# Forgetting attention with the keys' running sums used as loaded: the causal mask from one GpSimd selection per tile, and the row of reciprocal sums stored from ScalarE's queue

## The chip, the core and the metric

The kernel runs on one core of one Trainium2 chip. The metric is the device time of one execution in microseconds (us); the kernel before takes 1107.3 us (median of three runs, 1104.75 to 1107.84).

The core has five engines, each with an instruction queue of its own: TensorE (PE in the profile, with its weight loads as PEld), VectorE (DVE), ScalarE (ACT), GpSimd (POOL) and SyncE (SP), which here only issues DMAs. Each engine works through its queue in order, and semaphores tie the queues together.

## The reference, cut to what matters

The program is one decoder block on a sequence of 1024 tokens of width 1024: an input projection, attention with a forget gate beside a branch of chunked spatial gating (gMLP), an output projection, then a gated feed-forward layer with a short convolution. The change lies in the attention, which has 8 heads of dimension 64:

```python
c = jnp.cumsum(log_f, axis=1)                 # log_f = log_sigmoid(forget gate)
logits = einsum('bqhd,bkhd->bhqk', qi, k) * scale
logits = logits + ci[..., None] - c_k         # running sum of the query minus that of the key
logits = jnp.where(causal, logits, -inf)
p = softmax(logits, axis=-1)
out = einsum('bhqk,bkhd->bqhd', p, v)
```

The softmax of a row does not change when one number is added to the whole row, so the term `ci` of the query can be left out of the computation without changing `p`.

## The kernel before

All large products are split into three passes of a high and a low part, and the projections use a Strassen-like scheme. One list of stages runs from top to bottom: input projections (to about 215 us of the profiled execution), attention together with the projection of the gMLP branch (about 222 to 410 us), then the feed-forward layer, in which TensorE runs without a pause until the end. Instructions of different stages are interleaved on the engines by a scheduler that works from the dependences; the code below says what depends on what, not the final order on each engine.

What the change touches, with the lines of the profile:

- **Constants, lines 124 to 131.** `ident` is a 128x128 identity in float32, `identb` its bfloat16 copy made by VectorE (line 127), `maskb` a bfloat16 tile that holds 3e38 above the diagonal and 0 elsewhere (a memset and one GpSimd selection, line 130). `maskb` is also used once in `forget` to build a triangular matrix.
- **`forget_sums`, lines 492 to 520.** It works out the running sums of the forget gates. `z` ends up as minus log_f, so the sums are minus the running sums of the reference. They are put into `ncq` (tokens on partitions, line 517), transposed by TensorE (line 518), copied out of PSUM by VectorE (line 519) into `rows` and stored by SP to `ncd` in DRAM (line 520), one row of 1024 numbers for each head. In the traces the instructions of this stage that go to VectorE and ScalarE are recorded with line 43, that of a helper which keeps their order.
- **`att_head`, lines 702 to 788**, called for heads 0 to 7. For a head it loads queries and keys (`A`, `B`, `B2`: high and low parts) and the row of running sums, spread over 128 partitions (`nck`, line 708). `nck` and `B2` are two halves of one tile with the tag `x2`, of which there are two; the loads of a head therefore wait until the head two before it has done with the tile.
- Inside, `i` runs over four pairs of query tiles, `j` over the two tiles of a pair. A query tile `j` has n = 128*(j+1) keys. GpSimd first fills the tile `t` (128 x n) with the running sum of the query minus that of the key (line 725). Then, in chunks of up to 512 keys: TensorE multiplies queries and keys into PSUM in two passes (lines 733, 734); in the chunk with the diagonal a third small matmul adds `maskb` (line 736, identity in bfloat16 as stationary operand); VectorE adds `t` to the PSUM and takes the running minimum in one instruction (line 738; the products carry a minus sign, so that a minimum takes the place of the softmax's maximum). ScalarE then takes the exponential of the whole tile with its sum (line 741).
- After that, the tile is transposed by TensorE in 128x128 blocks (line 755), split into high and low part by ScalarE and VectorE (lines 756, 757), and multiplied by the values (line 765). At four points of a head `filler` puts in products of the gMLP branch (lines 808 to 810), which keep TensorE busy while the softmax runs; they are used up in the third head (head 2).
- **The end of a head, lines 774 to 788.** The reciprocal of the 1024 row sums `rs` is transposed by TensorE (777), copied by ScalarE to `rt` (778), stored by SP to `rsd` in DRAM (779), and loaded back as one row spread over 64 partitions (780). For every second head the attention output is multiplied by that row (786; GpSimd for the first three pairs of heads, VectorE for the last) and split again (787, 788).

SP issues nearly all DMAs in one queue. An instruction that waits there holds up the loads behind it. GpSimd in this stretch does the fills of line 725, the low parts of the weights of the output projection (line 163), and lines 786 and 788.

## Time and profile before

| | |
|---|---|
| median of three runs | 1107.3 us (1104.75 to 1107.84) |
| the profiled execution | 1106.7 us |
| its span from first to last instruction | 1104.9 us |
| granted TensorE clock, mean over the span | 0.994 |
| instructions | 14551 |
| HBM traffic | 142 GB/s over the span |

How to read the rows. "L733 PE MATMUL" is a matmul of line 733. A group of instructions has its count (x96), its busy time in us, the mean duration of one in ns, and the idle time of the engine just ahead of it with what ended that idle time. The durations of matmuls overlap: they are pipelined, one starts well before the one ahead has ended, so that the distance from start to start, and not the duration, is what a matmul costs TensorE. The chain of waits is followed back from the last instruction: at each step to the instruction or transfer that released it. In rows of stretches the columns are the stretch in us, its length, and for each engine busy time and number of instructions, then the granted clock, the share of the DMA engines and GB/s.

### The profile page before, as it was taken

The page shows a single profiled execution, that of the slowest core. Times are in us where ns is not written, and L with a number is a line of the kernel's source. Part 1 is how long each engine was busy: PE and PEld are TensorE (multiplying, and loading weights), DVE is VectorE, ACT ScalarE, POOL GpSimd, SP SyncE. Part 2 cuts the span into 40 slices and gives each one's busy share as a digit, 9 for nine tenths or more (in the row PEclk, how much of TensorE's full clock was granted, in tenths as well). Part 3 has the DMA queues.
Part 4 walks back from the last instruction along what each step waited for, and adds up shares of the span by engine and source line. Part 5 has one row for each costly group of instructions (what it writes and reads, how often), then busy time and mean ns, then how long its engine had stood idle before and what let it go on. Part 6 is the DMA issues. An engine that isn't in the chain of part 4 may idle for free.

```text
span 1104.9 us, 14551 instructions
## 1 busy us (share of the span) xinstructions
PE 1076.5 (97%) x5077; PEld 882.7 (80%) x5077; DVE 899.3 (81%) x1357; ACT 572.7 (52%) x990; POOL 267.0 (24%) x205
## 2 busy tenths in 40 slices
PE   9999998999999999998999999999999999999997
PEld 6888787787887788776888888888888888888886
DVE  5985799774679868999899999999898875898774
ACT  5656543454468766663434444444435444444653
POOL 0002233133146441334333332323332000000000
PEclk9999999999999999999999999999999999999999
DMA  9242366846575335313223132323321899433342
GB/s 336 87 152 78 97 167 175 256 128 212 190 218 173 96 111 180 110 60 122 86 105 133 67 124 96 115 77 112 127 87 48 268 314 334 131 96 98 128 135 98
DMA packets 64714, 158.19 MB, mean 143 GB/s; under 512 B 7672, under 2 KB 7936, under 8 KB 64640
## 3 DMA queue, kind: packets, MB, share of 16 engines
q1 hardware_dynamic: 64480, 156.73, 43.8%
q8 instruction: 40, 0.66, 0.3%
q10 hardware_dynamic: 160, 0.53, 0.1%
q14 instruction: 34, 0.28, 0.1%
HBM read 114.95 MB, written 42.27 MB: 142 GB/s over the span
## 4 chain that ended last, share of the span: by engine, by line
PE 68%; DVE 8%; ACT 2%; DMA 2%; issue 2%; POOL 1%; SPq 0%; ACTq 0%; POOLq 0%; DVEq 0%
PE k L1195 18%; PE qa L1005 10%; PE qd L1005 10%; PE qc L1005 9%; PE qb L1005 5%; PE pb L765 3%; PE pb L755 2%; PE ps L260 2%; PE pf L808 1%; PE pf L809 1%; PE pf L810 1%; DVE whb L163 1%; DMA x<-ncd 1%; PE ps L733 1%; PE ps L734 1%
## 5 line engine op out<-in xcount | busy, mean ns | idle before, releaser
L1195 PE MATMUL k<-whb,wha 128*128 128x512 f32 x924 | 209.7, 389 | 0.0
L1195 PEld LDWEIGHTS k<-whb,wha 128*128 128x128 f32 x924 | 173.4, 188 | 36.1
L1005 PE MATMUL qa<-xB,wha 128*128 128x512 f32 x528 | 130.5, 397 | 4.4 <-DVE wha L163 4.4
L1005 PE MATMUL qc<-xT,whb 128*128 128x512 f32 x540 | 130.2, 390 | 1.3 <-DVE xT L936 1.3
L1005 PEld LDWEIGHTS qa<-xB,wha 128*128 128x128 f32 x528 | 101.0, 192 | 26.4 <-DVE wha L163 5.3
L1005 PEld LDWEIGHTS qc<-xT,whb 128*128 128x128 f32 x540 | 101.1, 188 | 23.2 <-DVE xT L936 1.7
L157 ACT CAST wha<-sg 128x512 fp32r<-128x512 f32 x77 | 47.9, 622 | 99.5 <-PE k L1195 85.8
L157 ACT CAST whb<-sg 128x512 fp32r<-128x512 f32 x85 | 52.0, 616 | 71.6 <-PE qc L1005 69.5
L163 DVE TENSOR_TENSOR wha<-sg,wha 128x512 fp32r<-128x512 f32 x77 | 52.8, 687 | 41.2 <-ACT wha L157 41.1
L163 DVE TENSOR_TENSOR whb<-sg,whb 128x512 fp32r<-128x512 f32 x85 | 62.9, 742 | 9.1 <-ACT whb L157 8.9
L1005 PE MATMUL qd<-xB,whb 128*128 128x512 f32 x264 | 63.9, 389 | 0.1
L1005 PE MATMUL qd<-xT,whb 128*128 128x512 f32 x264 | 63.4, 389 | 0.0
L765 PE MATMUL pb<-pt,V 128*128 128x256 f32 (+1 forms) x320 | 59.0, 299 | 3.4 <-ACT pt L756 2.7
L1005 PE MATMUL qb<-xT,whb 128*128 128x512 f32 x252 | 61.0, 389 | 1.0 <-DVE whb L163 1.0
L756 ACT CAST pt<-pb 128x512 fp32r<-128x512 f32 (+1 forms) x80 | 41.2, 543 | 38.6 <-PE pb L755 37.8
L1005 PEld LDWEIGHTS qd<-xB,whb 128*128 128x128 f32 x264 | 49.6, 188 | 10.8 <-issue 0.5
L757 DVE TENSOR_TENSOR pt<-pb,pt 128x512 fp32r<-128x512 f32 (+1 forms) x80 | 48.3, 633 | 12.2 <-ACT pt L756 11.9
L893 POOL TENSOR_TENSOR sg<-sg,raw 128x512 f32<-128x512 f32 x21 | 42.5, 2023 | 64.5 <-issue 63.4
L1005 PEld LDWEIGHTS qd<-xT,whb 128*128 128x128 f32 x264 | 49.5, 188 | 10.3
L765 PEld LDWEIGHTS pb<-pt,V 128*128 128x128 f32 x320 | 47.2, 190 | 13.1 <-ACT pt L756 8.2
L892 POOL TENSOR_TENSOR sg<-raw 128x512 f32<-128x512 f32 x21 | 30.6, 1457 | 110.0 <-DVE whb L163 98.1
L1005 PEld LDWEIGHTS qb<-xT,whb 128*128 128x128 f32 x252 | 47.2, 188 | 11.1 <-DVE whb L163 1.4
(381 smaller groups left out, 2347.9 us busy)
## 6 DMA issues: line engine op xcount, KB each, us to landing
raw<-wup SPq DMA_DIRECT2D x44, 512.0 KB, 3.6
sg<-hx SPq DMA_DIRECT2D x77, 256.0 KB, 2.8
hx<-hs SPq DMA_DIRECT2D x44, 256.0 KB, 2.0
hx<-ca SPq DMA_DIRECT2D x33, 256.0 KB, 2.0
xT<-wdn SPq DMA_DIRECT2D x28, 256.0 KB, 4.9
raw<-wqk SPq DMA_DIRECT2D x8, 512.0 KB, 3.9
qd<-G SPq DMA_DIRECT2D x16, 256.0 KB, 4.0
kd<-G SPq DMA_DIRECT2D x16, 256.0 KB, 3.2
```

Source lines behind the costliest of these rows:

```text
L157: act.copy(h, src)
L163: return eng.tensor_tensor(out=l, in0=src, in1=f32(h), op=ALU.subtract)
L260: pe.matmul(banks[m], xs(n, xi, k)[:, ms], w[:, wi, :], start=(first and k == 0 and c == 0), stop=(k == 3 and c == 2), skip_group_check=True)
L733: pe.matmul(ps[:, 0:e - c], A[:, qs], B[:, c:e], start=True, stop=False)
L755: pe.transpose(ptr[:, c:c + P], tj[jj][:, k * P:(k + 1) * P], ident)
L756: act.copy(pt[:, 0, 0:w], ptr[:, 0:w])
L757: dve.tensor_tensor(out=pt[:, 1, 0:w], in0=ptr[:, 0:w], in1=f32(pt[:, 0, 0:w]), op=ALU.subtract)
L765: pe.matmul(po[:, oo:oo + n], lhs, pt[:, s, o:o + n], start=(k == 0 and s == 0), stop=(s == 1 and half))
L892: pool.tensor_tensor(out=s[0], in0=a21, in1=a22, op=ALU.add)
L893: pool.tensor_tensor(out=s[1], in0=s[0], in1=a11, op=ALU.add)
L1005: pe.matmul(ps, w[:, wi, ks], xb[:, xi, k, :], start=(first and n == 0), stop=(n == 11), skip_group_check=True)
L1195: pe.matmul(banks[bk + m], xh[:, xi, ms], wh[:, wi, :], start=(first and p_ == 0 and n == 0), stop=(p_ == NP - 1 and n == 2), skip_group_c ...
```

## The change

Three edits.

1. The running sums of the keys enter the softmax as they are loaded. `forget_sums` writes its sums to `z` instead of `ncq`, and the copy out of PSUM moves from VectorE to ScalarE, where it also turns the sign (scale -1). The row in DRAM is then already what has to be added to the product, and the query's term is left out.
2. GpSimd's fill is replaced by one selection (`affine_select`) per query tile. It writes only the chunk that has the diagonal (columns c0 to n, with c0 = 0 for j < 4 and 512 for j >= 4): the running sums where the key is not after the query, 3e38 elsewhere. VectorE reads this chunk from `t` and the other chunk, which j >= 4 have, straight from the loaded row `ck`. The small matmul with `maskb` is gone, and so are `identb` and `ncq`.
3. The store of `rt` to `rsd` is issued by ScalarE instead of SP.

```diff
-    identb = cst.tile([P, P], BF16, name="identb")
-    dve.tensor_copy(identb, ident)
...
-        dve.tensor_tensor(out=ncq, in0=v3(ps[:, 64:128]), in1=run, op=ALU.add)
-        pe.transpose(ps[0:64, 192:320], ncq.rearrange("p h t -> p (h t)"), ident)
-        dve.tensor_copy(rows, ps[0:64, 192:320])
+        dve.tensor_tensor(out=v3(z), in0=v3(ps[:, 64:128]), in1=run, op=ALU.add)
+        pe.transpose(ps[0:64, 192:320], z, ident)
+        act.activation(rows, ps[0:64, 192:320], AF.Copy, scale=-1.0)
...
-                pool.tensor_scalar(out=t, in0=nck[:, 0:n], scalar1=-1.0, scalar2=ncq[:, h, j:j + 1],
-                                   op0=ALU.mult, op1=ALU.add)
+                c0 = (j // 4) * 512
+                pool.affine_select(out=t[:, c0:n], in_=ck[:, c0:n], pattern=[[-1, n - c0]], compare_op=ALU.is_ge,
+                                   fill=BIG, base=j * P - c0, channel_multiplier=1)
...
-                    last = e == n
...
-                    pe.matmul(ps[:, 0:e - c], A[:, qs], B2[:, c:e], start=False, stop=not last)
-                    if last:
-                        pe.matmul(ps[:, e - c - P:e - c], identb, maskb, start=False, stop=True)
+                    pe.matmul(ps[:, 0:e - c], A[:, qs], B2[:, c:e], start=False, stop=True)
...
-                    dve.tensor_tensor_reduce(out=t[:, c:e], in0=ps[:, 0:e - c], in1=t[:, c:e], scale=1.0,
+                    dve.tensor_tensor_reduce(out=t[:, c:e], in0=ps[:, 0:e - c], in1=(t if c == c0 else ck)[:, c:e], scale=1.0,
...
-        sp.dma_start(out=rsd[h], in_=rt)
+        act.dma_start(out=rsd[h], in_=rt)
```

The scheduler's order changes with it in places. On GpSimd the four selections of head 5's first two pairs now stand ahead of the multiplication of line 786 for the second pair of heads, where the four fills stood behind it. On SP the load of line 780 for head 3 now stands behind the first two loads of head 6, and that for head 4 behind the first load of head 7.

More of the change, by code (lines that the diff above doesn't have):

```diff
@@ L138, in block_kernel @@
     ss1 = cst.tile([P, 8], F32, name="ss1")
-    ncq = cst.tile([P, 8, 8], F32, name="ncq")
     qd = drm.tile([8, 2, 64, 1024], F32, name="qd")
@@ L704, in att_head @@
         ab, nb = sb("x1", [P, 2, 1024], F32R), sb("x2", [P, 2, 1024], F32R)
-        A, B, nck, B2 = ab[:, 0, :], ab[:, 1, :], f32(nb[:, 0, :]), nb[:, 1, :]
+        A, B, ck, B2 = ab[:, 0, :], ab[:, 1, :], f32(nb[:, 0, :]), nb[:, 1, :]
         sp.dma_start(out=f32(A), in_=qd[h].rearrange("s d t -> (s d) t"))
         sp.dma_start(out=f32(B), in_=kd[h].rearrange("s d t -> (s d) t"))
-        sp.dma_start(out=nck, in_=ncd[h:h + 1, :].to_broadcast((P, 1024)))
+        sp.dma_start(out=ck, in_=ncd[h:h + 1, :].to_broadcast((P, 1024)))
         sp.dma_start(out=f32(B2[0:64, :]), in_=kd[h, 1])
```

## The prediction

> **What bounds the kernel now.** I read the head of the page first, then the attention stage in three stretches, then the chain of waits in each.

> ```profile
> span 1104.9 us, 14551 instructions
> PE 1076.5 (97%) x5077; PEld 882.7 (80%) x5077; DVE 899.3 (81%) x1357; ACT 572.7 (52%) x990; POOL 267.0 (24%) x205
> ```

> TensorE is busy 97% of the span and GpSimd 24%: work taken from TensorE can shorten the kernel, work taken from GpSimd only where something waits for GpSimd. The edits lie in the attention, so this stage decides.

> ```profile
> 222.00:318.00 96.00, 95.01 (x531) 76.54 (x529) 60.51 (x144) 47.25 (x99) 36.50 (x41) 1.00 0.56 173
> 318.00:340.00 22.00, 19.99 (x147) 16.99 (x146) 18.61 (x51) 16.27 (x40) 7.35 (x10) 1.00 0.88 269
> 340.00:400.00 60.00, 56.96 (x398) 49.40 (x399) 50.54 (x135) 50.65 (x111) 36.85 (x35) 0.97 0.34 108
> ```

> In the first 96 us TensorE is busy 95.01 us, VectorE 60.51 and ScalarE 47.25: a plain TensorE bound, with the gMLP products as filling. In the next 22 us the DMA engines are at 0.88, TensorE misses 2 us. In the last 60 us TensorE misses 3 us, while VectorE and ScalarE are each busy 50.5 us: the softmax's chain through all engines. What sets the end shows in the chain, one row by line for each stretch, in order:

> ```profile
> by line: PE pf L808 14.2%; PE pf L809 14.0%; PE pf L810 13.6%; PE pb L765 13.6%; PE pb L755 10.1%; PE ps L733 6.2%; PE ps L734 5.3%; POOL whl L163 5.1%; PE pb L680 4.2%; PE pb L667 1.7%; PE pb L666 1.7%; PE pb L665 1.5%; DVE pt L757 1.5%; P
> by line: DMA x<-ncd 47.9%; DVE t L738 11.5%; issue 8.9%; DVE pt L757 8.2%; POOL t L725 4.5%; ACT H L741 3.8%; DVE H L772 3.1%; PE pb L765 3.1%; POOL H L725 2.3%; ACT pt L756 2.2%; SPq L707 1.9%; PE ps L734 1.6%; ACT t L741 1.2%; PE ps L736
> by line: PE pb L765 25.0%; PE pb L755 15.4%; POOL H L786 7.6%; PE ps L734 6.7%; PE ps L733 6.4%; DMA H<-rsd 5.9%; ACT pt L756 5.0%; DVE pt L757 4.9%; issue 3.9%; POOL H L725 3.5%; DVE t L738 2.4%; DVE H L772 2.2%; DMA rsd<-t 2.0%; ACT G L78
> ```

> First stretch: almost all TensorE. Second: half is the load of head 4's running sums, and TensorE hardly appears. Third: the four TensorE lines shown make 25.0 + 15.4 + 6.7 + 6.4 = 53.5%.

> **The change, part by part. The 64 mask matmuls.** Their group, and where they lie in the same stretches (instructions of line 736 alone):

> ```profile
> L736 PE MATMUL ps<-maskb,identb 128*128 128x128 bf16 x64 | 14.7, 230 | 0.0
> 222.00:318.00 96.00, 5.26 (x23) 2.21 (x23) 1.00 0.56 173
> 318.00:340.00 22.00, 2.98 (x13) 1.25 (x13) 1.00 0.88 269
> 340.00:400.00 60.00, 6.46 (x28) 2.79 (x28) 0.97 0.34 108
> ```

> The 14.7 us are durations, which overlap. A start-to-start reading needs one place in order of time, and two rows for spacing without a mask:

> ```profile
> 249.09 0.34 PE L734 MATMUL ps<-x,x 128*128 128x384 f32 x1
> 249.27 0.23 PE L736 MATMUL ps<-maskb,identb 128*128 128x128 bf16 x1
> 249.31 0.48 PE L733 MATMUL ps<-x 128*128 128x512 f32 x1
> 249.63 0.40 PE L734 MATMUL ps<-x,x 128*128 128x512 f32 x1
> ...
> 232.52 0.39 PE L809 MATMUL pf<-whl,G 128*128 128x512 f32 x1
> 232.75 0.40 PE L810 MATMUL pf<-whl,G 128*128 128x512 f32 x1
> ...
> 243.61 0.93 PE L755 MATMUL pb<-ident,H 128*128 128x128 f32 x7
> ...
> L755 PE MATMUL pb<-ident,H 128*128 128x128 f32 x80 | 12.8, 274 | 0.3 <-DVE H L772 0.3
> ```

> With the mask, the stretch from L734 to the next L734 is 0.54 us. Without it, L734 takes 0.18 (to 249.27) and the 512-column L733 0.23 (spacing of the gMLP products): 0.41. The mask costs 0.13 us, though the matmul behind it starts only 0.04 later: the rest appears as 0.32 instead of 0.23 on that next one, whose weights have no long matmul to be loaded under. The seven transposes give the same size: (0.93 - 0.27)/6 = 0.11 us each, 0.27 being the duration of one, from the last row. Bounds per mask: 0.04 (its own start spacing) and 0.23 (its duration); I take 0.13, which is measured across both neighbours.

> First stretch: 23 x 0.13 = 3.0 us, counted in full. Second: 13 masks, counted at nothing; the 10.54 us DMA below hides them, and what TensorE finishes earlier it waits longer. Third: 28 x 0.13 = 3.6, of which the 53.5% TensorE share gives 1.9. Together 4.9; with full cover lost or won, 3.0 to 8.3.

> [...]

> **GpSimd's selections.**

> ```profile
> L725 POOL TENSOR_SCALAR t<-x,ncq 128x896 f32<-128x896 f32 (+3 forms) x32 | 32.0, 1012 | 70.0 <-PE pb L755 39.7 <-PE ps L260 20.1 <-PE ps L736 10.2
> L725 POOL TENSOR_SCALAR H<-x,ncq 128x128 f32<-128x128 f32 (+3 forms) x32 | 16.6, 535 | 24.9 <-DMA x<-ncd 18.9 <-PE ps L734 6.0
> L658 POOL TENSOR_SCALAR_AFFINE_SELECT pt<-pt 128x1024 f32<-128x1024 f32 x1 | 1.6, 1552 | 0.0
> L130 POOL TENSOR_SCALAR_AFFINE_SELECT maskb<-maskb 128x128 bf16<-128x128 bf16 x1 | 0.3, 292 | 0.0
> ```

> The fills cost 48.6 us. A selection takes 292 ns at 128 columns and 1552 at 1024, so 1.41 ns a column: 292, 472, 652, 832 for the four widths, 16 of each, 36.0 us. Widths are now at most 512, so the long tiles gain and the 384 and 512 ones lose 0.1 us. Bounds: nothing gained on the path, and the stands of TensorE that these fills touch:

> ```profile
> 319.18 10.54 DMA x<-ncd
> 330.71 1.00 POOL t L725
> 331.74 0.75 DVE t L738
> ...
> 348.74 2.17 POOL H L786
> 351.11 2.07 POOL H L725 x4
> ```

> After the late load the chain passes a fill of 1.00 us and then the minimum. The minimum of a long tile's first chunk now waits for the load alone; the 128-column fill ahead is shorter as well. I count 0.8 of this 1.00. At 351.11 four fills stand behind line 786, which waits for the row of sums; in the new order they stand ahead of it. I count 0.5 of their 2.07, since VectorE, busy five sixths of that stretch, is late next. Together 1.3, between 0 and 3.1. The idle 70 and 25 us in the rows above say that elsewhere GpSimd waits for others.

> New waits: the half tile of running sums is now read by VectorE too, so the load two heads later waits for it. Behind that load on SP stand the two loads of low keys. The reader is a minimum of some 0.75 us just behind the products on which the first load of that head waits anyway; 0 to 0.75 us, once, on the late load; I take 0.1.

> **ScalarE's queue.**

> ```profile
> L43 ACTq DMA_DIRECT2D rbd<-pt x1: 539/539/539, 110.6 to 110.6; - x1
> L779 SPq DMA_DIRECT2D rsd<-t x8: 289/296/357, 262.6 to 407.3; - x8
> 343.55 0.25 ACT t L778
> 343.82 1.21 DMA rsd<-t
> PEld pb L765 <- ACT pt L756: 8.2, 24, 1.7
> PE pb L765 <- ACT pt L756: 2.7, 6, 1.6
> ```

> An issue takes 0.296 us on SP and took 0.539 on ScalarE: eight stores hold ScalarE 2.4 to 4.3 us. On SP the store follows the copy by 0.02 us (343.55 + 0.25 to 343.82), so nothing is gained there, and the reload behind it on SP waits for the store's landing as before. Behind the store on ScalarE stand the casts of line 756, for which TensorE waits 8.2 + 2.7 us in all. Six of the eight stores (heads 2 to 7) come when the gMLP filling is used up; 6 x 0.4 x a quarter = 0.6 us lost, the quarter lying between ScalarE's few per cent of the chain and the whole; bounds 0 and 4.3.

> **The rest.** VectorE loses the cast of the identity and the copy of the rows; the latter goes to ScalarE:

> ```profile
> 132.83 0.28 DVE L43 COPY gg<-ps 64x128 f32<-64x128 f32 x1 [0.20 <-PE ps L518]
> 134.94 0.62 ACT L43 CAST G<-G 128x512 fp32r<-128x512 f32 x1 [1.83 <-DVE G L43]
> ```

> ScalarE stands idle 1.83 us just there, so some 0.3 us costs nothing (0.3 without that cover). Nothing reads the row before the attention. Sum: 4.9 + 1.3 - 0.1 - 0.6 = 5.5 us. The profiled execution took 1106.7, so 1101.2; the median of the runs lies 0.6 above it. Predicted: **1101.2 us**.

> **Rivals.**

> *More comes through.* If VectorE and ScalarE keep up, all 41 later masks count: 8.3, and 1.00 + 1.0 of GpSimd's two waits, give 1096.4. For: TensorE misses only 5 us of 82 in the two later stretches. Against: the chain's 46% outside TensorE.

> *The gain is eaten.* Only the first stretch counts, each mask by the smaller spacing, and the chain of loads, minima and exponentials keeps its length: 23 x 0.11 = 2.5, less 0.6 on ScalarE: 1104.8. For: the 10.54 us load and 50.5 us of VectorE and ScalarE in 60. Against: that load starts when TensorE has ended earlier work, so it moves forward too.

> *ScalarE stands at the store: slower.* If the store must first wait for an older transfer with which it shares a completion count, ScalarE stands until that has landed, with exponentials and casts behind it. Place: heads 2 to 7. Price: the load of 10.54 us shows what a transfer may take; 4 us at each of three stores, less 2 us that overlap with other waits, is 10 against a gain of 5.5: 1111. It decides once ScalarE stands over 5.5 us on the path in all. Against: on SP the store went 0.02 us after the copy, with no such wait. [...]

> *The selection isn't what it seems.* If a selection costs twice the line above, GpSimd needs 72 us instead of 49 in a stage where it has 100 idle; this gives the time of the second rival.

> **How the numbers follow.** Forecast 0.60, more 0.10, eaten 0.21 (the slow selection in it), slower 0.09. About 0.3%, 3.3 us, is what a measurement can tell from no change: under 1103.4 is faster. The forecast's own case lies a little on both sides of that bound: 0.55 of its 0.60 below; with the 0.10, faster 0.65, same 0.26, slower 0.09. The range runs from 1096.5, where more comes through, to 1107.0, where the eaten case ends with its bounds used up; the slower case and a sliver of the first are left out.

> **What would show it.** Line 736 gone from TensorE; start spacing of 0.23 from L734 to a following 512-column matmul. The stage from 222 to 318 shorter by 3 us, the load of running sums for head 4 issued that much earlier, at some 316. Selections of 292 to 832 ns, 36 us in all. ScalarE's issues of `rsd` of 0.3 to 0.54 us without a wait ahead. From the start of the dense feed-forward matmuls to the end no difference. I am wrong if the first stretch keeps its length, if TensorE's idle time after 318 grows by as much as the masks take away, or if ScalarE shows idle time ahead of the stores.

## The result, and the profile after

The changed kernel takes 1099.91 us (median of 12 runs, 1096.46 to 1104.16) against 1108.44 us for the kernel before (median of 12 beside them, 1104.69 to 1110.71). The ratio is 0.9928, with a 95% interval of 0.9912 to 0.9944: 8.0 us faster (6.2 to 9.8). The profiled execution took 1102.1 us, 4.5 less than the one before.

The head of the page after:

```profile
span 1100.4 us, 14437 instructions
PE 1070.2 (97%) x5013; PEld 880.7 (80%) x5013; DVE 897.8 (82%) x1355; ACT 572.2 (52%) x991; POOL 248.6 (23%) x205
```

64 matmuls are gone and GpSimd is busy 18.4 us less. The three stretches of the prediction, in the kernel after (stretch, length, PE, PEld, DVE, ACT, POOL busy with counts, granted clock, DMA share, GB/s):

```profile
222.00:318.00 96.00, 95.03 (x526) 77.13 (x525) 62.70 (x153) 48.53 (x104) 29.22 (x39) 1.00 0.56 179
318.00:340.00 22.00, 19.60 (x129) 17.44 (x128) 17.58 (x48) 15.75 (x39) 3.37 (x8) 0.92 0.81 234
340.00:400.00 60.00, 55.26 (x376) 48.49 (x375) 50.19 (x133) 50.68 (x111) 30.27 (x36) 0.97 0.38 108
```

From 318 on TensorE misses 2.40 + 4.74 = 7.1 us, where it missed 2.01 + 3.04 = 5.1 before, and in the middle stretch the granted clock is 0.92 in place of 1.00, which is worth 22 x 0.08 = 1.8 us. Together 2.1 + 1.8 = 3.9 us: not far below what the 41 later masks can have cost there at 0.11 us each (4.5). That comes near one of the signs by which the prediction said it would be wrong, TensorE's idle time growing by as much as the masks take away; by idle time alone it is 2.1 us.

Fixed stretches mix work that has moved, so I cut by the work itself: **part 1** from the last transposition of the gMLP input (232.0 before, 231.1 after) to the last product of the gMLP branch (x64), **part 2** from there to the last product with the values (x320). The view of a single line gives the cuts (count, min/median/max ns, first to last start), before and after:

```profile
L810 PE MATMUL pf<-whl,G x64: 387/393/445, 232.7 to 313.7; 128*128 128x512 f32 x64
L765 PE MATMUL pb<-pt,V x320: 220/282/415, 237.7 to 408.0; 128*128 128x256 f32 x128, 128*128 128x128 f32 x32
```
```profile
L804 PE MATMUL pf<-whl,G x64: 387/390/445, 231.8 to 310.8; 128*128 128x512 f32 x64
L759 PE MATMUL pb<-pt,V x320: 218/282/580, 236.7 to 404.7; 128*128 128x256 f32 x128, 128*128 128x128 f32 x32
```

The two parts, before, then after:

```profile
232.00:313.70 81.70, 80.71 (x444) 65.32 (x443) 47.13 (x113) 38.69 (x83) 24.52 (x27) 1.00 0.58 180
313.70:408.00 94.30, 88.92 (x622) 76.26 (x621) 77.72 (x202) 74.83 (x165) 50.53 (x50) 0.98 0.45 140
```
```profile
231.10:310.80 79.70, 78.77 (x427) 64.00 (x425) 47.22 (x113) 38.20 (x83) 19.04 (x27) 1.00 0.55 179
310.80:404.70 93.90, 86.75 (x583) 76.20 (x582) 76.68 (x202) 73.91 (x164) 38.50 (x50) 0.96 0.49 141
```

Ahead of part 1: 0.9 us earlier. Part 1, with 18 masks, is 2.0 us shorter at a full clock in both: 0.11 us a mask. Part 2, with 42 masks, is 0.4 us shorter, while its clock went from 0.98 to 0.96. Behind part 2 the rest is 1.2 us shorter (696.9 to 695.7); the clock can account for that, since in the clock's record one half-clock stretch of 3.4 us lies behind part 2 after the change (from 519.35) and two lay there before (from 500.31 and 524.21), not counting the last 6 us of each. That is the profiled pair's 4.5; the medians differ by more.

**Where part 2 loses.** TensorE has two stands in the kernel after, with a bracket that names the idle time and its releaser:

```profile
330.50 0.62 PE L759 MATMUL pb<-pt,V 128*128 128x256 f32 x3 [2.06 <-DVE pt L751]
354.09 0.39 PE L759 MATMUL pb<-pt,V 128*128 128x256 f32 x1 [2.25 <-ACT pt L750]
```

And the stretches in and behind them, in the columns given above:

```profile
328.20:330.50 2.30, 0.24 (x4) 0.01 (x2) 1.29 (x4) 0.63 (x1) 2.30 (x6) 1.00 0.37 107
331.80:335.20 3.40, 3.06 (x14) 2.92 (x14) 3.37 (x10) 1.79 (x3) 0.43 (x2) 0.52 0.73 228
...
351.80:354.00 2.20, 0.03 (x1) 0.00 (x0) 0.27 (x2) 1.49 (x3) 2.20 (x6) 1.00 0.18 47
355.70:359.10 3.40, 3.40 (x17) 3.21 (x16) 2.63 (x8) 1.24 (x4) 2.40 (x3) 0.53 0.00 0
```

Each of these stands of about 2 us is followed, 1.1 and 1.4 us later (330.50 to 331.62, 354.09 to 355.51), by 3.41 us at half the clock (0.52 and 0.53 in the rows, which begin a little later). TensorE is busy for 3.06 and 3.40 of the rows' 3.40 us and does about half the work: two 512-column products start 0.43 us apart there (357.07 and 357.50) and 0.23 us behind (360.43 and 360.66). So a stand costs its own 2 us and, by an estimate from these rows, up to 1.7 more, half of 3.41. Not every stand is followed by one (last section). Before, there was one such pair in part 2, with 0.5 us between (383.75 to 384.26):

```profile
382.00:383.70 1.70, 0.19 (x2) 0.05 (x1) 0.58 (x2) 1.63 (x3) 1.70 (x5) 1.00 0.00 0
384.10:387.50 3.40, 3.40 (x17) 3.14 (x16) 2.52 (x9) 3.24 (x7) 3.40 (x3) 0.52 0.00 0
```

The causes of the two stands of the kernel after stand on other engines. First stand: GpSimd, then VectorE.

```profile
328.07 0.65 POOL L722 TENSOR_SCALAR_AFFINE_SELECT H<-x 128x128 f32<-128x128 f32 x2 [12.40 <-DMA x<-ncd]
328.67 1.07 POOL L722 TENSOR_SCALAR_AFFINE_SELECT t<-x 128x384 f32<-128x384 f32 x2
...
329.21 0.62 DVE L732 CUSTOM_DVE_ANT_0 t<-ps,t,mn 128x384 f32<-128x384 f32 x1 [2.56 <-POOL t L722]
```

The first two selections are head 4's, which wait for the late load; the next two are for the last pair of head 3, whose row had been there long before. They stood behind the others in GpSimd's queue, and VectorE's minimum waited 2.56 us for them. This order isn't new. In the kernel before, head 4's first two fills wait for the same load and head 3's last two (896 and 1024 columns) stand behind them:

```profile
329.88 0.83 POOL L725 TENSOR_SCALAR H<-x,ncq 128x128 f32<-128x128 f32 x2 [10.38 <-DMA x<-ncd]
330.69 2.11 POOL L725 TENSOR_SCALAR t<-x,ncq 128x896 f32<-128x896 f32 x2
```

There VectorE waited 1.70 us for GpSimd at 331.74, and TensorE had two short stands, 0.68 and 1.00 us, with no half clock behind them. So the change kept this place, and what was new is one long stand in place of two short ones. Second stand: SP, GpSimd, ScalarE.

```profile
342.62 0.33 SPq L702 DMA_DIRECT2D x<-qd  x1
342.99 0.43 SPq L703 DMA_DIRECT2D x<-kd  x1
343.52 0.45 SPq L774 DMA_DIRECT2D H<-rsd  x1
...
350.11 2.36 POOL L780 TENSOR_TENSOR H<-H 128x1024 f32<-128x1024 f32 x1 [6.51 <-DMA H<-rsd]
...
352.51 1.04 ACT L781 CAST A<-H 128x1024 fp32r<-128x1024 f32 x1 [1.73 <-POOL H L780]
```

The reload of head 3's row (L774) goes out at 343.52 behind two loads of head 6, and GpSimd, which waits for it, starts to multiply 6.6 us later; ScalarE stands 1.73 us ahead of the cast of that product, and the cast that TensorE waits for (L750) stands behind it on ScalarE. Before, the reload went out at 345.04, ahead of head 6's loads, and the multiplication began 3.7 us later (348.74). So the reload takes longer too, 6.43 us against 3.54 in the chains of waits, with the two loads under way; which of the two, the place in the queue or the slower transfer, makes the stand isn't shown. The order on SP was in the front part of this document; no term of the prediction priced it.

### The profile page after: what moved, and what is told of

It reads as the page before. It is cut to its first block, busy times and chain, and to the rows that moved or that the text cites. A ratio compares the mean times of both kernels' runs of the same rounds, so it can differ in the third digit from the quotient of the medians.

```text
span 1100.4 us, 14437 instructions
## 1 busy us (share of the span) xinstructions
PE 1070.2 (97%) x5013; PEld 880.7 (80%) x5013; DVE 897.8 (82%) x1355; ACT 572.2 (52%) x991; POOL 248.6 (23%) x205
## 4 chain that ended last, share of the span: by engine, by line
PE 69%; DVE 7%; ACT 3%; issue 2%; DMA 2%; POOL 1%; SPq 0%; ACTq 0%; POOLq 0%; DVEq 0%
PE k L1189 18%; PE qa L999 10%; PE qd L999 10%; PE qc L999 10%; PE qb L999 5%; PE pb L759 3%; PE ps L256 2%; PE pb L749 2%; PE pf L803 1%; PE pf L804 1%; PE pf L802 1%; DMA x<-ncd 1%; PE ps L730 1%; PE ps L729 1%; DVE whb L159 1%
## 5 line engine op out<-in xcount | busy, mean ns | idle before, releaser
L153 ACT CAST wha<-sg 128x512 fp32r<-128x512 f32 x77 | 47.9, 622 | 97.8 <-PE k L1189 87.0
L759 PEld LDWEIGHTS pb<-pt,V 128*128 128x128 f32 x320 | 48.3, 194 | 18.6 <-ACT pt L750 11.5
L750 ACT CAST pt<-pb 128x512 fp32r<-128x512 f32 (+1 forms) x80 | 40.8, 545 | 33.4 <-PE pb L749 32.7
L751 DVE TENSOR_TENSOR pt<-pb,pt 128x512 fp32r<-128x512 f32 (+1 forms) x80 | 48.2, 632 | 10.9 <-ACT pt L750 10.2
L886 POOL TENSOR_TENSOR sg<-raw 128x512 f32<-128x512 f32 x21 | 30.6, 1458 | 110.0 <-DVE whb L159 85.6
```

The source lines that it names most:

```text
L153: act.copy(h, src)
L750: act.copy(pt[:, 0, 0:w], ptr[:, 0:w])
L751: dve.tensor_tensor(out=pt[:, 1, 0:w], in0=ptr[:, 0:w], in1=f32(pt[:, 0, 0:w]), op=ALU.subtract)
L759: pe.matmul(po[:, oo:oo + n], lhs, pt[:, s, o:o + n], start=(k == 0 and s == 0), stop=(s == 1 and half))
L886: pool.tensor_tensor(out=s[0], in0=a21, in1=a22, op=ALU.add)
```

## The experiments

Two theories. **A** (the prediction's): the masks' 4.9 us are most of the gain. **B**: the masks are worth nothing, in part 1 either, and the gain comes from GpSimd's shorter fills and from minima that no longer wait for them. Each kernel was compared with the kernel before in five rounds. The changed kernel wasn't run again in these rounds, so that a difference between it and an experiment is a difference of two ratios, uncertain by about 2.5 us. "Time x clock" is the median over a kernel's runs of its time multiplied by its mean granted clock: what the run would take at full clock throughout, roughly, since the clock has three digits (0.0005 is 0.55 us). The row "before" is that of e1 to e4; beside e5 to e8 the kernel before had a mean clock of 0.9926 and 1099.4 us at full clock, beside e9 to e12 0.9929 and 1100.3.

| kernel | ratio to before (95%) | median us | mean clock | time x clock |
|---|---|---|---|---|
| before (23 runs) | 1 | 1107.4 | 0.9937 | 1099.8 |
| after (12 runs) | 0.9928 (0.9912 to 0.9944) | 1099.9 | 0.9937 | 1093.1 |
| e1_neutral_mask | 0.9937 (0.9918 to 0.9955) | 1099.9 | 0.9948 | 1094.5 |
| e2_before_no_mask | 1.0005 (0.9993 to 1.0017) | 1107.4 | 0.9918 | 1098.3 |
| e4_before_two_masks | 1.0015 (1.0003 to 1.0027) | 1108.9 | 0.9949 | 1102.8 |
| e3_store_on_sp | 0.9950 (0.9933 to 0.9967) | 1101.5 | 0.9930 | 1094.1 |
| e5_full_width | 0.9960 (0.9945 to 0.9975) | 1103.1 | 0.9920 | 1094.6 |
| e6_select_order | 0.9916 (0.9898 to 0.9934) | 1097.8 | 0.9940 | 1091.7 |
| e7_reload_first | 0.9966 (0.9952 to 0.9979) | 1104.0 | 0.9912 | 1094.4 |
| e8_cast_on_gpsimd | 0.9942 (0.9922 to 0.9962) | 1101.8 | 0.9923 | 1093.3 |
| e9_late_neutral | 0.9929 (0.9910 to 0.9948) | 1099.6 | 0.9938 | 1093.0 |
| e10_rows_on_scalar | 0.9985 (0.9969 to 1.0002) | 1105.8 | 0.9933 | 1099.3 |
| e11_order_and_cast | 0.9936 (0.9919 to 0.9954) | 1100.6 | 0.9927 | 1091.7 |
| e12_order_late_neutral | 0.9917 (0.9898 to 0.9935) | 1098.2 | 0.9940 | 1091.4 |

### The masks alone, in both directions

e1: the changed kernel with 64 masks that add zero.

```diff
+    identb = cst.tile([P, P], BF16, name="identb")
+    dve.tensor_copy(identb, ident)
+    zerob = cst.tile([P, P], BF16, name="zerob")
+    dve.memset(zerob, 0.0)
...
-                    pe.matmul(ps[:, 0:e - c], A[:, qs], B2[:, c:e], start=False, stop=True)
+                    pe.matmul(ps[:, 0:e - c], A[:, qs], B2[:, c:e], start=False, stop=e < n)
+                    if e == n:
+                        pe.matmul(ps[:, e - c - P:e - c], identb, zerob, start=False, stop=True)
```

> The changed kernel, with the 64 small matmuls put back as neutral ones (bfloat16 identity times a tile of zeros, so nothing is added to the logits; the selection still masks). Theory A, TensorE's spacing: each is worth 0.13 us, in full in the stage with the gMLP products and half of it behind, 4.9 us in all. The ratio to the kernel before goes from 0.993 to about 0.997 (1105 us), and the stretch from the last spatial-gating product to the last gMLP output product, 87.7 us before and 85.6 after, comes back to 87.5 to 88.5. Rival B, GpSimd: the gain came from shorter fills and from minima that no longer wait for them. Then the ratio stays at 0.993 and the stretch at 85.6.

e2: the kernel before without its masks (no causal mask is left in it).

```diff
-                    pe.matmul(ps[:, 0:e - c], A[:, qs], B2[:, c:e], start=False, stop=not last)
-                    if last:
-                        pe.matmul(ps[:, e - c - P:e - c], identb, maskb, start=False, stop=True)
+                    pe.matmul(ps[:, 0:e - c], A[:, qs], B2[:, c:e], start=False, stop=True)
```

> The kernel before without its 64 mask matmuls; the causal mask is left out of the computation, everything else stays, GpSimd's fills too. Theory A: 4.9 us faster, ratio 0.9956 (0.9935 to 0.997), the stretch with the gMLP products 85 us. Rival B: ratio 1.000, the stretch as before, 87.7 us.

e4: the kernel before with each mask in two halves.

```diff
-                       fill=BIG, base=0, channel_multiplier=1)
+                       fill=BIG / 2, base=0, channel_multiplier=1)
...
                     if last:
+                        pe.matmul(ps[:, e - c - P:e - c], identb, maskb, start=False, stop=False)
                         pe.matmul(ps[:, e - c - P:e - c], identb, maskb, start=False, stop=True)
```

> The kernel before with each mask matmul done twice (half of the large number each time). Theory A: 64 more at 0.11 to 0.13 us, covered as the first ones: 5 us slower, ratio 1.0045 (1.003 to 1.007), the gMLP stretch 90 us. If a mask costs only its own start spacing of 0.04 us: ratio 1.001, the stretch 88.5 us. Rival B: 1.000 to 1.001.

Parts 1 and 2 of the three, in this order, from the view of stretches:

```profile
231.40:312.70 81.30, 80.38 (x444) 65.30 (x443) 47.09 (x113) 38.72 (x83) 19.22 (x27) 1.00 0.56 179
312.70:403.30 90.60, 88.40 (x625) 75.55 (x624) 78.29 (x202) 73.74 (x164) 38.56 (x50) 1.00 0.48 145
```
```profile
231.70:311.40 79.70, 78.88 (x426) 64.01 (x424) 47.10 (x113) 38.15 (x83) 24.46 (x27) 1.00 0.59 187
311.40:409.90 98.50, 88.34 (x580) 77.14 (x579) 77.06 (x202) 74.57 (x165) 50.78 (x50) 0.95 0.45 132
```
```profile
232.10:315.90 83.80, 82.24 (x463) 66.34 (x462) 47.34 (x113) 38.81 (x83) 24.54 (x27) 1.00 0.55 177
315.90:411.60 95.70, 91.63 (x668) 77.70 (x667) 78.15 (x202) 74.81 (x165) 50.56 (x50) 1.00 0.46 140
```

Part 1 answers each time: with the 18 masks 81.3 (e1) and 81.7 (before), without them 79.7 (e2) and 79.7 (after), with 36 83.8 (e4). Part 2 does not: without masks it is longer (98.5 in e2 at a clock of 0.95, 93.9 in the kernel after at 0.96), with masks e1 has 90.6 at 1.00. The whole: e1 is 0.0009 above the changed kernel (1.0 us, well within the 2.5), e2 gains nothing (0.9993 to 1.0017: between a gain of 0.8 and a loss of 1.9 us), e4 loses 1.7 us. So theory A is out: no removal of masks gives 4.9 us. B as it stood is out too, since part 1 answers. At full clock the masks show as 1.4 us in e1, 1.5 in e2 and 3.0 in e4, near what part 1 gives; e2 hands it back as clock, 0.9918 against 0.9937, which is 2.1 us. For the 1.9 us that the prediction took from its third stretch, e2 is the test: part 1 is 2.0 us shorter and the whole gains 0.8 us at most, so what lies outside part 1 gave nothing and lost at least 1.2 us (at full clock, 0.5).

e9 puts the neutral masks of e1 into heads 3 to 7 only; the early ones are out.

```diff
+                    pe.matmul(ps[:, 0:e - c], A[:, qs], B2[:, c:e], start=False, stop=e < n or h < 3)
+                    if e == n and h >= 3:
+                        pe.matmul(ps[:, e - c - P:e - c], identb, zerob, start=False, stop=True)
```

> The changed kernel with the neutral mask matmuls only from head 3 on, where the gMLP products are used up; heads 0 to 2 have none. Theory D: a mask costs TensorE 0.09 us while the gMLP products fill it, and nothing behind, where TensorE's stands of 2 us and more are each followed by 3.4 us at half the clock, which the extra matmuls prevent. Then the stretch from the last transposition of the gMLP branch to its last output product is 79.7 us (as in the changed kernel), the late heads up to the last product with the values take 90.6 (as with all neutral masks, without a halved clock in them), and the ratio is 0.991 to 0.9925. If the neutral masks helped by a lucky order alone: 0.994.

0.9929 against 0.9928 for the changed kernel: the later masks cost nothing that these intervals (2.5 us to each side) can show, and they save nothing either. The trace agrees with theory D on the two parts, 79.4 and 90.5 us, both at a clock of 1.00. The runs don't show its reason, that the extra matmuls prevent the half clock: the mean clock is 0.9938, that of the changed kernel 0.9937. e12, below, gives the same a second time (0.9917 against 0.9916).

### GpSimd's selection

e5: one selection over the full width of the tile; a long tile's first chunk is then read from `t`, so its minimum waits for GpSimd as in the kernel before. The second chunk of a long tile reads the loaded row, so it has no mask in this kernel; the wording below, that all minima read the tile, is right for the first chunks alone.

```diff
-                c0 = (j // 4) * 512
+                c0 = 0
```

> The changed kernel with the selection over the whole width of a tile (128 to 1024 columns) and all minima reading the tile, as before the change; no mask matmuls. GpSimd's part in the attention goes from 36 to 59 us by the line of 1.41 ns a column, and the first chunk of a long tile waits for GpSimd again. Theory C, formed after the first four runs (the masks are worth 2 to 3 us at most, the rest comes from GpSimd's shorter and decoupled work in the late heads, where each stand of TensorE is followed by a stretch at half the clock): the gain is mostly lost, ratio 0.997 to 1.000. If the gain came from neither the masks nor GpSimd but from the new order alone: ratio 0.993.

0.9960 against 0.9928: 3.5 us of the 8.0 are gone, less than theory C forecast, with intervals that just don't overlap (0.9945 to 0.9975, 0.9912 to 0.9944). At full clock the difference is 1.5 us (1094.6 against 1093.1); the rest of the 3.5 goes with the lower mean clock, 0.9920. The groups of the selection, after and in e5:

```profile
L722 POOL TENSOR_SCALAR_AFFINE_SELECT t<-x 128x384 f32<-128x384 f32 (+3 forms) x32 | 15.1, 491 | 80.2 <-PE pb L749 50.9 <-PE ps L256 20.6 <-ACT t L735 8.7
L722 POOL TENSOR_SCALAR_AFFINE_SELECT H<-x 128x128 f32<-128x128 f32 (+3 forms) x32 | 13.6, 452 | 25.8 <-DMA x<-ncd 25.8
```
```profile
L722 POOL TENSOR_SCALAR_AFFINE_SELECT t<-x 128x896 f32<-128x896 f32 (+3 forms) x32 | 28.7, 920 | 74.0 <-PE pb L749 40.3 <-DMA x<-ncd 20.7 <-PE ps L730 6.6
L732 DVE CUSTOM_DVE_ANT_0 t<-ps,t,lim 128x512 f32<-128x512 f32 x32 | 23.7, 746 | 4.7 <-POOL t L722 3.9 <-PE ps L730 0.9
```

The second row of e5 is the minimum of the long tiles' first chunk, which now waits 3.9 us for GpSimd. The wide selections are also 13.6 us longer in sum. Which of the two, length or wait, makes the 3.5 us, this run doesn't say.

### The store

```diff
-        act.dma_start(out=rsd[h], in_=rt)
+        sp.dma_start(out=rsd[h], in_=rt)
```

> The changed kernel with the store of the reciprocal sums back on SP. As predicted (the store holds ScalarE 0.4 us, a quarter of it on the path): 0.6 us faster than the changed kernel, ratio 0.9922. As the trace after the change reads (the issue of 0.273 us runs beside the cast ahead of it, so it holds nothing): ratio 0.993, within the noise of the changed kernel; TensorE's waits for the casts unchanged at 16 us in all, unless the scheduler's order changes with it.

The changed kernel with the store back on SP is slower by 0.0022 (2.4 us, 1.0 at full clock; the intervals overlap, so a gain from ScalarE's queue is likely and not settled). The loss of 0.6 us that the prediction took lies outside what the intervals allow. The edit doesn't isolate the store: TensorE's waits for the casts, which were to stay at 16 us, are 9.1 us in its trace against 16.3, and head 3's reload goes out behind one load of head 6 (at 341.29) and not two. Its profiled execution took 1100.7 us, less than the 1102.1 of the changed kernel, so no trace shows where 2.4 us would come from. The eight issues, after and in e3, and the one for head 3 in ScalarE's order of time:

```profile
L773 ACTq DMA_DIRECT2D rsd<-t x8: 269/273/287, 261.8 to 405.0; - x8
```
```profile
L773 SPq DMA_DIRECT2D rsd<-t x8: 290/296/341, 262.0 to 401.4; - x8
```
```profile
341.22 0.25 ACT L772 COPY t<-pb 8x128 f32<-8x128 f32 x1
341.37 0.47 ACT L750 CAST pt<-pb 128x384 fp32r<-128x384 f32 x1
341.50 0.27 ACTq L773 DMA_DIRECT2D rsd<-t  x1
```

The store is issued at 341.50, within the cast that runs from 341.37 to 341.84, and 0.03 us behind the copy's end: no wait ahead of it, and no stand of ScalarE. Of the eight issues none has idle time ahead of it.

### The copy of the rows

The kernel before, with this one copy on ScalarE.

```diff
-        dve.tensor_copy(rows, ps[0:64, 192:320])
+        act.copy(rows, ps[0:64, 192:320])
```

> The kernel before with one part of the change: the copy of the running sums out of PSUM goes to ScalarE. TensorE's stand of 1.07 us at 173 us, which the kernels with the whole change do not show, should go if this copy's place in VectorE's order causes it: 0.9 us less, ratio 0.999. As predicted (it costs nothing and gives nothing): ratio 1.000 and the stand stays.

0.9985, or 1.7 us, with an interval that reaches 1.0002. The trace shows 0.8 us, and where: TensorE, before and in e10.

```profile
174.45 3.00 PE L404 MATMUL qd<-t,whl 128*128 128x512 f32 x12 [0.91 <-DVE G L43]
```
```profile
173.58 3.00 PE L404 MATMUL qd<-t,whl 128*128 128x512 f32 x12
```

A projection's product no longer waits 0.91 us for VectorE at 174, some 40 us behind the copy: in e10, as in the changed kernel, the order that the scheduler makes of VectorE's work is another one from about 141 us on. The attention then begins 0.8 us earlier (last transposition at 231.2 against 232.0, 231.1 in the changed kernel).

### The two stands in part 2

e6 holds the selections on GpSimd in the order of the heads; nothing else in the code is new.

```diff
+    sels = []
...
-                pool.affine_select(out=t[:, c0:n], in_=ck[:, c0:n], pattern=[[-1, n - c0]], compare_op=ALU.is_ge,
+                sel = pool.affine_select(out=t[:, c0:n], in_=ck[:, c0:n], pattern=[[-1, n - c0]], compare_op=ALU.is_ge,
                                    fill=BIG, base=j * P - c0, channel_multiplier=1)
+                if sels:
+                    after(tc, sel, sels[-1])
+                sels.append(sel)
```

> The changed kernel with the selections held in the order of the heads on GpSimd; nothing else changes its place on any engine. In the trace after the change, two selections of head 4 wait for their load until 328.07 us with two of head 3 behind them; VectorE stands 2.56 us for one of those, TensorE 2.2 us, and a stretch at half the clock begins there. If that stand is on the path: 2 us less, or 3.5 with the clock, ratio 0.990. If head 4's load ends the wait anyway: 0.993.

0.9916, the lowest of all, 1097.8 us; its interval overlaps that of the changed kernel (1099.9; 1.3 us by the ratios, 2.1 by the medians), so that it is better is possible and not shown. In its trace head 3's selections run at 321.95, ahead of head 4's and of the load that these wait for; the second stand is 1.67 us; and part 2 is 88.2 us at a clock of 1.00. One row each of GpSimd and TensorE in order of time, and part 2:

```profile
321.95 1.09 POOL L723 TENSOR_SCALAR_AFFINE_SELECT t<-x 128x384 f32<-128x384 f32 x2 [6.04 <-PE pb L775]
```
```profile
350.42 0.39 PE L763 MATMUL pb<-pt,V 128*128 128x256 f32 x1 [1.67 <-ACT pt L754]
```
```profile
311.00:399.20 88.20, 84.21 (x583) 73.46 (x582) 76.44 (x202) 73.61 (x164) 38.81 (x50) 1.00 0.50 150
```

The first stand is gone, and no half clock follows the second. That is one execution: over the runs the mean clock is 0.9940, hardly above the changed kernel's 0.9937.

e7 holds the first load of head h on SP behind the reload of head h-3, against the second stand.

```diff
-        sp.dma_start(out=f32(A), in_=qd[h].rearrange("s d t -> (s d) t"))
+        first = sp.dma_start(out=f32(A), in_=qd[h].rearrange("s d t -> (s d) t"))
+        if h >= 3:
+            after(tc, first, reloads[h - 3])
...
-        sp.dma_start(out=attF[p][hh * 64:hh * 64 + 64, 1, :],
-                     in_=rsd[h].rearrange("a b -> (a b)").unsqueeze(0).to_broadcast((64, 1024)))
+        reloads.append(sp.dma_start(out=attF[p][hh * 64:hh * 64 + 64, 1, :],
+                     in_=rsd[h].rearrange("a b -> (a b)").unsqueeze(0).to_broadcast((64, 1024))))
```

> The changed kernel with the reload of the reciprocal sums held ahead of the loads of the head three further on SP, as the order was before the change. In the trace after the change the reload of head 3 is issued 1.8 us after its store has gone out, behind two loads, and lands 6.6 us after its issue (3.5 before); GpSimd, then ScalarE's cast, then TensorE (2.4 us at 351.6) wait for it, and the clock is halved there. If so: 2 to 3.5 us less, ratio 0.990. If the loads of head 6 are late in exchange, or the cast waits for GpSimd as long: 0.993.

Slower than the changed kernel by 0.0038, 4 us. It didn't make what it was meant to:

```profile
345.03 0.33 SPq L706 DMA_DIRECT2D x<-kd  x1
345.45 1.83 SPq L777 DMA_DIRECT2D H<-rsd  x1
347.34 0.58 SPq L703 DMA_DIRECT2D x<-qd  x1
```

Another load of head 6, which the edit doesn't hold, was pulled ahead of the reload; the reload goes out at 345.45, later than the 343.52 of the changed kernel, and head 6's other loads later still. TensorE's stands there are longer than in the changed kernel, 3.50 us (to 332.73) and 2.82 us (to 354.32). What an early reload would be worth stays open.

e8 takes the cast of line 781 off ScalarE; e11 has the edits of e6 and e8; e12 those of e6 and e9.

```diff
-                act.copy(attT[p][:, 0, o], f[:, 0, o])
+                (pool.tensor_copy if p < 3 else act.copy)(attT[p][:, 0, o], f[:, 0, o])
```

> The changed kernel with the cast of the scaled attention output (high part, first three pairs of heads) on GpSimd in place of ScalarE. In the trace after the change ScalarE stands 1.73 and 1.13 us ahead of that cast and takes 1.05 for it, with the casts of the transposed tiles behind; TensorE stands 2.4 and 1.4 us. If ScalarE's queue is what passes the wait on: 2 to 4 us less, ratio 0.990. If GpSimd, which takes some 1.2 us more for each cast, is late with the selections in exchange: 0.993 or above.

> The changed kernel with the selections in the order of the heads, and the cast of the scaled output on GpSimd for the first three pairs. The order alone left two stands of TensorE, 1.84 us at 348 and 0.85 at 376, both at the cast in ScalarE's queue. If both are the cast's: 2 us less than the order alone, ratio 0.989 to 0.990. If GpSimd's longer queue takes its place: 0.992.

> The changed kernel with the selections in the order of the heads and the neutral mask matmuls from head 3 on. Theory D: the order alone has no halved stretch in the late heads any more (88.2 us there), so that the extra matmuls can only cost: 41 times 0.04 to 0.09 us partly covered, 0 to 2 us above the order alone, ratio 0.9915 to 0.9935. If extra matmuls help for another reason than the clock: below 0.9905.

e8: 0.9942, no gain, though in its profiled execution part 2 is 88.3 us without a half clock; the mean clock over its runs is 0.9923. e11: 0.9936, so the two edits don't add. e12: 0.9917, the same as e6, with the same mean clock of 0.9940, though in its trace part 2 is 90.9 us at a clock of 1.00, where e6 had 88.2. At full clock e6 and e12 have 1091.7 and 1091.4, 1.4 to 1.7 under the changed kernel.

## Why the prediction was right in its number and wrong in its main step

The time came within 1.3 us (1101.2 forecast, 1099.9 measured) and the direction held. The gain was larger than forecast, 8.0 us (6.2 to 9.8) against 5.5, and it did not come for the reason that carried most of the sum. That the total lies so near is luck: a large term that mostly didn't come was made up for by terms that had been put too low or at nothing.

- **The masks, 4.9 us: the step that failed.** A mask's price was near: 0.13 forecast, 0.11 measured in part 1 ((81.7 - 79.7)/18; e4 gives 2.1/18 = 0.12). The place where it was read gives nearly the forecast number again: without the mask, the step from one L730 to the next is 0.17 + 0.23 = 0.40 us, 0.14 less than the 0.54 with it.

```profile
248.14 0.33 PE L730 MATMUL ps<-x,x 128*128 128x384 f32 x1
248.31 0.40 PE L729 MATMUL ps<-x 128*128 128x512 f32 x1
248.54 0.39 PE L730 MATMUL ps<-x,x 128*128 128x512 f32 x1
```

  What failed is the third stretch's 1.9 us, for which TensorE's 53.5% of the chain was taken as the share that comes through. Taken from the kernel before (e2), the masks outside part 1 give no gain but lose at least 1.2 us; put back into the changed kernel (e9, e12), the late ones cost nothing that can be measured, though 1.9 us would lie within those intervals. A reading that fits, and isn't shown, is that where TensorE is paced by the softmax's chain a matmul less is a longer stand. Only the first stretch's term is real: 2.0 us in part 1 (3.0 forecast for the wider stretch), and of that about 1 us appears in the whole (e1), none in e2.
- **GpSimd's selections, 1.3 us forecast.** e5 gives 3.5 us for the narrow selection with its decoupled first chunk, 1.5 of it at full clock, so the term was too low or about right. The selections take 15.1 + 13.6 = 28.7 us, not 36.0: the line drawn through the 1552 ns of L658 was too steep. The place of the 0.8 us was misread: the fill of 1.00 us at 330.71 belongs to head 3's last pair, whose row had long been there, and behind the late load the chain still passes GpSimd, since the second chunk's selection waits in the same queue. From the end of that load to the minimum it went from 2.02 us (329.72 to 331.74) to 1.26 (327.95 to 329.21), which is the 0.8, by shorter selections and not by the decoupled chunk.
- **The new waits, 0.1 us.** Not seen. The load of head 4's running sums is issued at 316.42, 0.47 us behind the load ahead of it (315.95), the same distance as before (318.71 to 319.18). The forecast said 316, which came true, though 0.9 of the 2.76 us had been gained ahead of the masks. The load itself took 11.53 us, 10.54 before.
- **The store on ScalarE, -0.6 us: wrong in sign by what e3 shows, or nothing.** The issues take 0.27 us, just under the range of 0.3 to 0.54, and run beside a cast or right behind the copy, not as a stand ahead of the next cast.
- **The copy of the rows, 0.** Its cover held, and it still brought 0.8 us in the trace, since VectorE's later work stands in another order.
- **Not in the sum:** the order on SP, which was in the front part and which the second stand of part 2 hangs on, and the half clock. The order behind the first stand was there before the change; e6 puts undoing it at 1.3 us, give or take 2.5.

The rivals. *More comes through* is out: in e2 the later masks are worth nothing. *The gain is eaten* was right on the masks and wrong on the sum, since it allowed nothing for GpSimd. *ScalarE stands at the store* is out: no wait ahead of any of the eight stores. *The selection isn't what it seems* is out: 28.7 us, not 72.

What adds up to 8.0: by the ratios 1.0 (masks, e1) + 3.5 (selection, e5) + 2.4 (store, e3) + 1.7 (rows, e10) = 8.6, each uncertain by 2 us or more. At full clock the same four are 1.4 + 1.5 + 1.0 + 1.0 = 4.9, of 1099.8 - 1093.1 = 6.7. So the nearness of 8.6 to 8.0 shows neither the parts nor that none is missed: each edit also changes the order on the queues, and what the clock costs differs between kernels that do the same work, 6.1 us in e6 and 9.6 in e7 (median less time x clock). How the 8.0 us divide among shorter selections, the decoupled chunk, the store and the order stays open. Why the profiled pair differs by 4.5 us only: without the end, the execution after had four half-clock stretches (from 195.09, 331.62, 355.51 and 519.35), worth up to 1.7 us each, and the one before three. That the clock is what sets runs of 1096.5 and 1104.2 us apart fits their mean clocks of 0.997 and 0.991, and wasn't tested further.

## What to carry to other kernels

Price a removed instruction only in the stages that its engine bounds; where the engine already stands, take nothing for it, and look at what stands longer. Read the order that a scheduler makes of the queues as part of the change, and compare it with the order before: in the trace after the change, selections and a reload that waited behind others went with stands of 2 us of TensorE and a slower clock behind them (0.52 and 0.53 over 3.4 us), and one of the two orders was old. Put the granted clock beside each time: two of the differences here are half as large or less at full clock.

## What the runs showed of the hardware

**Issues on ScalarE** took 0.27 us (median of the eight, in the kernel after). Four of them ran within a cast or an exponential, as the one at 341.50 within the cast from 341.37 to 341.84, and the other four 0.03 us behind the end of the copy; the one issue before, of 0.54 us, had not shown this. **Selections in float32** on GpSimd at 128 partitions took 292 ns at 128 columns, 613 and 737 at 512 (into two different tiles, in the kernel after), and 1168 at 1024 (e5): 0.8 to 1.2 ns a column beyond the first 128. The selection at L658 of the kernel before took 1552 at 1024; its pattern has two dimensions, and whether that is why isn't shown.

```profile
L722 POOL TENSOR_SCALAR_AFFINE_SELECT t<-x 128x512 f32<-128x512 f32 x8 | 5.9, 737 | 0.0
L722 POOL TENSOR_SCALAR_AFFINE_SELECT H<-x 128x512 f32<-128x512 f32 x8 | 4.9, 613 | 0.0
```
```profile
L722 POOL TENSOR_SCALAR_AFFINE_SELECT t<-x 128x1024 f32<-128x1024 f32 x8 | 9.3, 1168 | 0.0
```
